# Feed-forward part of a transformer layer: where the rounding of each weight tile is traced, and two instructions that it is put behind

## The chip, the cores and the metric

One Trainium2 chip, one core. The metric is the device time of one execution in microseconds (us), the median of several runs. The profile comes from one further execution, which has its own time.

## The reference, cut to what matters

The program is one trunk layer for 640 tokens (128 context tokens, 512 latent ones) of 1024 features, in fp32: modulation from a conditioning vector, a combined input projection, grouped-query attention and neighbourhood attention, a merge, an output projection, a feed-forward part with squared ReLU, and a final norm. The change lies in the feed-forward part and the norm that ends the program:

```python
def _mlp(h, w_mlp_in, w_mlp_out):            # 1024 -> 4096 -> 1024
    return jnp.square(jax.nn.relu(h @ w_mlp_in)) @ w_mlp_out
...
h2 = _rmsnorm(x, n2) * (1 + sc2) + sh2
x = x + g2 * _mlp(h2, w1, w2)
...
y_sample = _rmsnorm(xs, final_norm_g)
```

## The kernel before, in words

**Layout.** Features lie on the 128 partitions, tokens on the free axis, in two halves of 320. An fp32 product is made of three fp32r products: each operand is a high part (a rounded copy) and a low part (the rest), and high by high, high by low and low by high are summed in one PSUM bank.

**The feed-forward part** takes the span from 557 us to about 906 us. It goes in four chunks c of 1024 hidden features. In a chunk both layers use a scheme of seven block products for a two by two block product: A11, A12, A22 and the combinations S1 to S4 of weight blocks, for n = 0 to 3 (of layer 1 the outputs, of layer 2 the pairs of output feature tiles x1_2n and x1_2n+1). The list `SEQ` (from the hand-written FIRST1, FIRST0, FIRST2, L1350 to L1366) names 196 products in the order in which they are traced. In a chunk's layer 2 that order ends S3(0..3), A22(0..3), S2(0..3), S1(0..3), S4(0..3). Each product is 12 matmuls of 128x128 by 320 columns (L1679 to L1681: high by high, high by low, low by high, four times).

**Weights.** A product's weight tile `wb` holds the high half in blocks 0 to 3 and the low half in blocks 4 to 7. Six such tiles exist, and `W.live` counts those in use. The class Operands (L1370 to L1441) fills them. `feed` loads fp32 tiles: `wst` for A11 and A12, and `wsb` for the rest, to which a GpSimd-issued DMA adds a second block of the matrix (L1401). `conv` rounds one weight: ScalarE copies to fp32r for the high half (L1416), then VectorE subtracts for the low half (L1421, for some products on GpSimd). For S4 of layer 2 in the last chunk, c = 3, ScalarE instead writes the negated weight into the low half (L1418), and a DMA issued by GpSimd adds the weight itself (L1419). After S3, S2 and A22 another GpSimd-issued DMA adds the next block into `wsb` (L1424), which forms the following combination. `ahead` rounds as long as fewer than six weights are live and the fp32 tile has been asked for.

**The main loop** (L1664 to L1709), for each product: get the weight, take a bank, 12 matmuls, then the evictions (`layer1` or `layer2`), then `W.live -= 1`, then the operands of layer 2 that have become complete (`operand` splits a hidden block into op, high on ScalarE at L1485 or L1488, low on VectorE at L1486 or L1489; `t_raw` forms sums of hidden blocks), then `ahead`, then a piece of side work. Before the loop `ahead` has rounded six weights, so that behind product i weight i+6 is rounded.

**Evictions in layer 2 of c = 3.** The bank is added with a gate into the residual tile x1 by VectorE (`gate_half`, L1532, one instruction or two, 128 and 192 columns), for S3, A22 and S2 by way of temporaries tp (L1599, L1602, L1605). When half of an x1 tile is complete, `done_half` squares it on ScalarE (L1547, tiles sq3 or acc3), adds the square to a running sum on VectorE (L1551), and scales x1 by the norm's weight on ScalarE (L1552). A half's norm is two matmuls with ones (L1559), a power on ScalarE and eight multiplications (L1568) with their output DMAs.

**What sets the order.** The program is traced in the order of the code, and the tile framework then orders each engine's instructions with its own estimates, the order of tracing as priority; so the order on an engine differs from that of the code. Within an engine instructions start in their order.

Of the kernel before, what the change touches and what calls it, by code (L numbers as in the profile page):

```python
# [74 lines left out]
def trunk_layer(ctx: ExitStack, tc: tile.TileContext, xT, small_in, wmodA, wmodB, tabs, cacheK, cacheV, bias,  # L75
                w_in, w_br, w_out, w1, w2, yT, akT, avT, bkT, bvT):
    nc = tc.nc
    PE, ACT, DVE = nc.tensor, nc.scalar, nc.vector
# [154 lines left out]
    def flush_later(todo=None):  # L233
        todo = later if todo is None else todo
        n = len(todo)
        for f in todo[:n]:
            f()
        del todo[:n]

    class Weights:  # L240
        def __init__(self):
            self.order = list(w_order())
            self.pos = {k: i for i, (k, _) in enumerate(self.order)}
            self.st, self.t = {}, {}
            self.nd = self.nc = self.live = self.busy = 0
            self.extra = self.defer = False
            self.behind = None
# [51 lines left out]
        def ahead(self):  # L299
            while self.nc < len(self.order):  # L300
                key = self.order[self.nc][0]
                if key in EXTRA and self.extra:
                    return
                if key not in EXTRA and self.live + 2 > 6:
                    return
                self.conv()
            if OPS:
                OPS[0].ahead()

    OPS = []  # L310
# [1059 lines left out]
    class Operands:  # L1370


        def __init__(self):
            self.st = {}
            self.loads = []
            for l, c, n, o in SEQ:
                k = (l, c, n, "A" if o in ("A11", "A12") else "B")
                if k not in self.loads:
                    self.loads.append(k)
            self.t = {}  # L1380
            self.nl = self.nc = 0
            self.busy = {"A": 0, "B": 0}

        def src(self, l, c, n, e):
            return (w1[8 * c + 2 * n + e] if l == 1 else w2[c, 2 * n + e]).rearrange("p (k n) -> p k n", k=KT)
# [46 lines left out]
        def ahead(self):  # L1432
            self.feed()
            while self.nc < len(SEQ) and W.live < 6 and (SEQ[self.nc][0], *SEQ[self.nc][1:3],
                                                         "A" if SEQ[self.nc][3] in ("A11", "A12") else "B") in self.st:
                self.conv()

        def get(self, x):
            while x not in self.t:
# [5 lines left out]
    def bank():  # L1445
        return pp8[0].tile([P, 512], F32, tag="b", bufs=8, name="b")[:, :HT]
# [22 lines left out]
    def opd(c, name):  # L1469
        if (c, name) not in OPD:  # L1470
            OPD[c, name] = (bp[0].tile([P, 8, HT], F32R, tag="op3", bufs=1, name="op") if len(OPD) % 3 == 2 else
                            m.tile([P, 8, HT], F32R, tag="op", bufs=2, name="op"))
        return OPD[c, name]
# [6 lines left out]
    def operand(c, name, ks=slice(0, 4)):  # L1480

        t, src = opd(c, name), hid_raw(c, {"B11": 11, "B21": 21, "T4": 21, "N22": 22}.get(name, 12))[:, ks]
        hi, lo = t[:, ks], t[:, 4 + ks.start:4 + ks.stop]
        if name == "N22":
            ACT.activation(hi, src, AF.Copy, scale=-1.0)  # L1485
            DVE.scalar_tensor_tensor(lo, src, -1.0, r32(hi), op0=OP.mult, op1=OP.subtract)  # L1486
        else:
            ACT.activation(hi, src, AF.Copy)  # L1488
            DVE.tensor_sub(lo, src, r32(hi))  # L1489

    def t_raw(c, name, ks=slice(0, 4)):

        b11, b12, b21, b22 = (hid_raw(c, b)[:, ks] for b in (11, 12, 21, 22))
        if name == "T3":
            DVE.tensor_sub(b12, b22, b12)
        elif name == "T2":
            DVE.tensor_add(b12, b12, b11)
        elif name == "T4":
            DVE.tensor_sub(b21, b21, b12)
        else:  # L1500
            DVE.tensor_sub(b12, b22, b12)
# [72 lines left out]
    def fold(n):  # L1574

        for h in range(2):
            gate_half(2 * n + 1, WS[n], h, neg)
# [58 lines left out]
    for n, h in todo:  # L1636
# [7 lines left out]
        e, i = n % 2, n // 2  # L1644
# [20 lines left out]
    for x in SEQ:  # L1665
        l, c, n, o = x
        w = OPS[0].get(x)
        if l == 1:
            xk = XN[o]
        else:  # L1670
            s = opd(c, XOF[o])
            xk = lambda k, s=s: (s[:, k], s[:, 4 + k])
        p = pairs.setdefault((l, c, n), Pair())
        whole = {"A12": "A11", "S1": "S2", "S4": "S2"}.get(o)
        b = getattr(p, "b" + whole) if whole else bank()
        setattr(p, "b" + o, b)
        for k in range(4):
            xh, xl = xk(k)
            PE.matmul(b, w[:, k], xh, start=not whole and k == 0, stop=False, skip_group_check=True)  # L1679
            PE.matmul(b, w[:, k], xl, start=False, stop=False, skip_group_check=True)  # L1680
            PE.matmul(b, w[:, 4 + k], xh, start=False, stop=o not in ("A11", "S2", "S1") and k == 3, skip_group_check=True)  # L1681
        (layer1 if l == 1 else layer2)(c, n, o, b, p)
        W.live -= 1
        if l == 1 and o in ("A12", "S2") and n > 1:
            operand(c, "B11" if o == "A12" else "B21", slice(0, 3) if n == 2 else slice(3, 4))
        if l == 1 and o == "S2":
            fold(n)
        if l == 1 and o == "S4" and n > 1:
            t_raw(c, "T3", slice(0, 3) if n == 2 else slice(3, 4))
        if l == 2:  # L1690
            if (o, n) == ("A11", 2):
                operand(c, "T3")
                t_raw(c, "T2")
                t_raw(c, "T4")
            if (o, n) == ("A11", 3):
                operand(c, "T4")
            if (o, n) == ("A12", 3):
                operand(c, "T2")
                t_raw(c, "T1")
            if (o, n) == ("S3", 3):  # L1700
                operand(c, "T1")
            if (o, n) == ("S2", 3):
                operand(c, "N22")
        OPS[0].ahead()
        flush_later()
        if side:
            side.pop(0)()
# [104 lines left out]
```

## Time and profile before

| what | value |
|---|---|
| time, median of 3 runs | 917.27 us (917.22 to 918.52) |
| profiled execution's own time | 917.51 us |
| its span in the trace | 915.7 us |
| mean granted TensorE clock | 0.997 |
| PE busy | 901.5 us, 98% of the span |
| VectorE (DVE) busy | 713.5 us, 78% |
| ScalarE (ACT) busy | 564.8 us, 62% |
| GpSimd (POOL) busy | 197.0 us, 22% |

Read it so: PE has hardly any idle time, so the other engines matter only where PE waits for them. "PEld" is the loading of a weight into PE, which overlaps the matmuls. In the timeline a row is one instruction, or several alike in a row (x2): start in us, busy us, engine, line, operation, output and inputs, count, and in brackets how long the engine was idle before it, with what ended that.

### The profile page before, as it was taken

The numbers are of one execution on the slowest core, as the hardware profiler recorded it, in microseconds if no ns is written. First come the engines' busy times: TensorE is split into PE (matmuls) and PEld (weight loads), VectorE is DVE, ScalarE is ACT, GpSimd is POOL, SyncE is SP. The second block draws the span as 40 slices with busy tenths as digits, with TensorE's granted clock in tenths as the row PEclk, the third lists the DMA queues.
The fourth block names the chain that finished last, engine by engine and source line by source line (L and its number), as shares of the span: only waits on it lengthen the run. The fifth ranks groups of instructions, "written<-read, shape, count | busy, mean of one in ns | idle before, by whom it ended". The sixth has DMA issues, their size and how long they took to land.

```text
span 915.7 us, 16620 instructions
## 1 busy us (share of the span) xinstructions
PE 901.5 (98%) x6120; PEld 871.5 (95%) x6120; DVE 713.5 (78%) x1508; ACT 564.8 (62%) x1176; POOL 197.0 (22%) x226
## 2 busy tenths in 40 slices
PE   9999999999999999999999999999999999999996
PEld 7799989999999999999999999999999999999995
DVE  6776887757666796767789996995798769976897
ACT  4566777756667765765325667537753576357765
POOL 0020200001211011211120000354244532454140
PEclk9999999999999999999999999999999999999998
DMA  9892400126645398999743463898778876898475
GB/s 348 317 266 69 113 24 26 62 72 159 161 119 125 120 284 256 249 268 251 251 140 100 116 165 105 134 210 186 186 122 191 178 174 144 180 173 182 97 126 151
DMA packets 54465, 151.09 MB, mean 165 GB/s; under 512 B 6704, under 2 KB 10432, under 8 KB 54384
## 3 DMA queue, kind: packets, MB, share of 16 engines
q1 hardware_dynamic: 31440, 99.74, 33.1%
q0 software_dynamic: 21792, 48.98, 30.8%
q10 hardware_dynamic: 1152, 1.31, 0.4%
q8 instruction: 48, 0.79, 0.4%
q14 instruction: 33, 0.27, 0.1%
HBM read 137.67 MB, written 4.60 MB: 155 GB/s over the span
## 4 chain that ended last, share of the span: by engine, by line
PE 81%; DVE 6%; DMA 5%; ACT 4%; issue 2%; POOL 0%; SPq 0%; DVEq 0%; ACTq 0%; POOLq 0%
PE b L1680 10%; PE b L1679 10%; PE b L1681 10%; PE pg L320 7%; PE pg L321 7%; PE pg L322 7%; PE pss L322 4%; PE pss L321 4%; PE pss L320 4%; DMA wsb<-w 2%; PE pt L321 2%; PE pt L322 2%; PE pt L320 2%; DMA ms<-wmodA 2%; PE pt L710 1%
## 5 line engine op out<-in xcount | busy, mean ns | idle before, releaser
L1416 ACT ACTIVATE wb<-wsb 128x512 fp32r<-128x512 f32 x140 | 87.1, 628 | 90.6 <-PE b L1681 59.2
L1680 PE MATMUL b<-op,wb 128*128 128x320 f32 x448 | 138.6, 309 | 0.7 <-DVE op L1489 0.7
L1679 PE MATMUL b<-op,wb 128*128 128x320 f32 x448 | 138.6, 309 | 0.0
L1681 PE MATMUL b<-op,wb 128*128 128x320 f32 x448 | 138.4, 309 | 0.0
L1421 DVE TENSOR_TENSOR wb<-wsb,wb 128x512 fp32r<-128x512 f32 x124 | 92.5, 749 | 26.5 <-ACT wb L1416 26.3
L1424 POOL DMA_DIRECT2D wsb<-w x84 | 74.4, 922 | 127.8 <-DVE wb L1421 99.7
L1123 DVE SCALAR_TENSOR_TENSOR mt<-wmt,cb 128x512 f32<-128x512 f32 x128 | 80.9, 686 | 6.0 <-DMA wmt<-wmodB 6.0
L1680 PEld LDWEIGHTS b<-op,wb 128*128 128x128 f32 x448 | 84.1, 188 | 1.2 <-DVE op L1489 1.2
L1679 PEld LDWEIGHTS b<-op,wb 128*128 128x128 f32 x448 | 84.1, 188 | 0.5 <-DVE x L1532 0.4
L1681 PEld LDWEIGHTS b<-op,wb 128*128 128x128 f32 x448 | 84.1, 188 | 0.0
L272 ACT ACTIVATE wh<-wst 128x512 fp32r<-128x512 f32 (+1 forms) x84 | 61.1, 739 | 32.1 <-PE pg L321 16.6
L1401 POOL DMA_DIRECT2D wsb<-w x28 | 26.0, 930 | 138.0 <-DVE xm L341 41.5
L281 DVE TENSOR_TENSOR wl<-wst,wh 128x512 fp32r<-128x512 f32 (+1 forms) x53 | 43.3, 821 | 14.9 <-ACT wh L272 12.8
L648 DVE TENSOR_TENSOR pl<-pt,ph 128x512 fp32r<-128x512 f32 (+1 forms) x72 | 44.9, 627 | 11.8 <-ACT ph L647 11.2
L647 ACT ACTIVATE ph<-pt 128x512 fp32r<-128x512 f32 (+1 forms) x72 | 39.2, 548 | 15.7 <-PE po L718 4.7
L1532 DVE SCALAR_TENSOR_TENSOR x<-b,parts,x 128x128 f32<-128x128 f32 (+1 forms) x116 | 46.3, 429 | 2.9 <-PE b L1681 2.2
L1416 ACT ACTIVATE wb<-wst 128x512 fp32r<-128x512 f32 x56 | 34.9, 626 | 17.1 <-PE b L1681 10.3
L1679 PE MATMUL b<-t,wb 128*128 128x320 f32 x144 | 44.7, 310 | 0.0
L1681 PE MATMUL b<-t,wb 128*128 128x320 f32 x144 | 44.5, 309 | 0.0
L1680 PE MATMUL b<-t,wb 128*128 128x320 f32 x144 | 44.5, 309 | 0.0
L1489 DVE TENSOR_TENSOR op<-hid,op 128x1280 fp32r<-128x1280 f32 (+2 forms) x32 | 37.0, 1155 | 7.6 <-ACT op L1488 7.4
L1532 DVE SCALAR_TENSOR_TENSOR x<-tp,parts,x 128x320 f32<-128x320 f32 (+2 forms) x60 | 38.9, 677 | 1.0 <-ACT tp L1583 1.0
(890 smaller groups left out, 3009.2 us busy)
## 6 DMA issues: line engine op xcount, KB each, us to landing
wsb<-w POOLq DMA_DIRECT2D x112, 256.0 KB, 5.1
wst<-w SPq DMA_DIRECT2D x36, 512.0 KB, 3.9
wmt<-wmodB SPq DMA_DIRECT2D x32, 512.0 KB, 5.5
wst<-w_in SPq DMA_DIRECT2D x31, 512.0 KB, 4.4
wsb<-w SPq DMA_DIRECT2D x28, 512.0 KB, 4.0
ms<-wmodA SPq DMA_DIRECT2D x16, 512.0 KB, 8.2
wl<-w_in POOLq DMA_DIRECT2D x10, 512.0 KB, 7.6
wst<-w_br SPq DMA_DIRECT2D x8, 512.0 KB, 4.2
```

The costliest lines, as they stand in the source:

```text
L272: ACT.activation(hi[:, ks], st[:, ks], AF.Copy)
L320: PE.matmul(ps, wh[:, k], xh[:, sl], start=first, stop=False)
L321: PE.matmul(ps, wh[:, k], xl[:, sl], start=False, stop=False)
L322: PE.matmul(ps, wl[:, k], xh[:, sl], start=False, stop=last)
L1123: DVE.scalar_tensor_tensor(t, st[:, q * 512:(q + 1) * 512], 1.0, r32(cb[2 * q + i][:, :512]), op0=OP.mult, op1=OP.mult, accum_out=parts[:, ...
L1416: ACT.activation(w[:, 0:4], t, AF.Copy)
L1421: (nc.gpsimd if o in BLKPOOL[l - 1] else DVE).tensor_sub(w[:, 4:8], t, r32(w[:, 0:4]))
L1424: nc.gpsimd.dma_start(t, self.src(l, c, n, e)[:, 4 * half:4 * half + 4], accum_op=OP.add)
L1532: DVE.scalar_tensor_tensor(X1[i][:, sl], src[:, sl.start - off:sl.stop - off], g[:, j:j + 1], X1[i][:, sl], op0=OP.mult, op1=OP.add)
L1679: PE.matmul(b, w[:, k], xh, start=not whole and k == 0, stop=False, skip_group_check=True)
L1680: PE.matmul(b, w[:, k], xl, start=False, stop=False, skip_group_check=True)
L1681: PE.matmul(b, w[:, 4 + k], xh, start=False, stop=o not in ("A11", "S2", "S1") and k == 3, skip_group_check=True)
```

## The change

Three edits in the feed-forward part's loop. `Operands` gets a list `behind`. Each `conv` that `ahead` makes is traced under an ordering context for each instruction in that list: what `conv` traces for an engine is put behind the listed instruction of that engine. And `ahead` is no longer called at the end of a product's turn but right after its evictions have been traced, with `behind` set to the last instruction traced until then on ScalarE and on VectorE; this is ahead of `W.live -= 1`, so that the count is still one higher, and behind product i it is weight i+5 that is rounded instead of weight i+6.

```diff
@@ class Operands, __init__
             self.busy = {"A": 0, "B": 0}
+            self.behind = []
@@ ahead
             while self.nc < len(SEQ) and W.live < 6 and (SEQ[self.nc][0], *SEQ[self.nc][1:3],
                                                          "A" if SEQ[self.nc][3] in ("A11", "A12") else "B") in self.st:
-                self.conv()
+                with ExitStack() as order:
+                    for i in self.behind:
+                        order.enter_context(tc.issue_after(i))
+                    self.conv()
@@ main loop, for x in SEQ
         (layer1 if l == 1 else layer2)(c, n, o, b, p)
+        OPS[0].behind = [next(i for i in reversed(nc.cur_bb.bb.instructions) if i.engine == e.engine) for e in (ACT, DVE)]
+        OPS[0].ahead()
         W.live -= 1
...
-        OPS[0].ahead()
         flush_later()
```

Lines after the first edit stand 1 further down in the changed kernel, from L1437 on 4 further (L1416 becomes L1417, L1547 becomes L1551), behind the third edit 6 or 5 further. All that is traced ahead of the loop keeps its order, and so do the loads that SyncE issues. Tiles of one name have other numbers in the two kernels.

The order on ScalarE near the end, in layer 2 of c = 3, before: the roundings of S1(3) (wb_10647), S4(0) (wb_10670), S4(1) (wb_10697) and S4(2) (wb_10717), with the first `done_half` behind S2, that of x1_1.

```order
L1416 ACTIVATE wb_10647<-wsb_10214 128x512
L1416 ACTIVATE wb_10670<-wsb_10205 128x512
L1418 ACTIVATE wb_10670<-wsb_10205 128x512
L1416 ACTIVATE wb_10697<-wsb_10208 128x512
L1418 ACTIVATE wb_10697<-wsb_10208 128x512
L1547 ACTIVATE sq3_10620<-x1_1_5742 128x320
L1552 ACTIVATE x1_1_5742<-x1_1_5742,pk_74 128x320
L1416 ACTIVATE wb_10717<-wsb_10211 128x512
```

The same place after, with S1(3) in wb_10667, S4(0) in wb_10690 and S4(1) in wb_10713:

```order
L1417 ACTIVATE wb_10667<-wsb_10230 128x512
L1551 ACTIVATE sq3_10686<-x1_7_6084 128x320
L1556 ACTIVATE x1_7_6084<-x1_7_6084,pk_74 128x320
L1417 ACTIVATE wb_10690<-wsb_10221 128x512
L1419 ACTIVATE wb_10690<-wsb_10221 128x512
L1551 ACTIVATE acc3_10710<-x1_1_5742 128x320
L1556 ACTIVATE x1_1_5742<-x1_1_5742,pk_74 128x320
L1417 ACTIVATE wb_10713<-wsb_10224 128x512
L1419 ACTIVATE wb_10713<-wsb_10224 128x512
```

S4(0)'s rounding stood ahead of all four `done_half` of S2, and now stands behind the last of them, that of x1_7; S4(1)'s stands behind the first square of the other half, which needs S1(0)'s eviction.

The order on VectorE around the evictions of S2, before: low halves of S1(0) to S1(3) (wb_10583, wb_10601, wb_10624, wb_10647) between the evictions of A22(2), S2(0) and S2(1) (the L1605 rows, banks b_10604 and b_10627).

```order
L1421 TENSOR_TENSOR wb_10583<-wsb_10205,wb_10583 128x512
L1602 TENSOR_TENSOR tp_10580<-b_10586,tp_10371 128x320
L1532 SCALAR_TENSOR_TENSOR x1_7_6084<-tp_10371,parts_3964,x1_7_6084 128x320
L1421 TENSOR_TENSOR wb_10601<-wsb_10208,wb_10601 128x512
L1605 TENSOR_TENSOR tp_10541<-tp_10541,b_10604 128x320
L1421 TENSOR_TENSOR wb_10624<-wsb_10211,wb_10624 128x512
L1532 SCALAR_TENSOR_TENSOR x1_1_5742<-tp_10541,parts_3964,x1_1_5742 128x128
L1532 SCALAR_TENSOR_TENSOR x1_1_5742<-tp_10541,parts_3964,x1_1_5742 128x192
L1605 TENSOR_TENSOR tp_10541<-tp_10541,b_10627 128x320
L1421 TENSOR_TENSOR wb_10647<-wsb_10214,wb_10647 128x512
```

The same place after: low halves of S1(0) (wb_10598) and S1(1) (wb_10621), and the evictions of S2(0) to S2(3) (banks b_10601, b_10624, b_10647, b_10670).

```order
L1422 TENSOR_TENSOR wb_10598<-wsb_10221,wb_10598 128x512
L1609 TENSOR_TENSOR tp_10537<-tp_10537,b_10601 128x320
L1609 TENSOR_TENSOR tp_10537<-tp_10537,b_10624 128x320
L1536 SCALAR_TENSOR_TENSOR x1_1_5742<-tp_10537,parts_3964,x1_1_5742 128x128
L1536 SCALAR_TENSOR_TENSOR x1_1_5742<-tp_10537,parts_3964,x1_1_5742 128x192
L1536 SCALAR_TENSOR_TENSOR x1_3_5901<-tp_10537,parts_3964,x1_3_5901 128x128
L1536 SCALAR_TENSOR_TENSOR x1_3_5901<-tp_10537,parts_3964,x1_3_5901 128x192
L1555 TENSOR_TENSOR acc3_10326<-acc3_10326,sq3_10617 128x320
L1609 TENSOR_TENSOR tp_10576<-tp_10576,b_10647 128x320
L1609 TENSOR_TENSOR tp_10576<-tp_10576,b_10670 128x320
L1422 TENSOR_TENSOR wb_10621<-wsb_10224,wb_10621 128x512
```

Three roundings, S1(1) to S1(3), stood ahead of the last two evictions of S2, and now stand behind them. In the rest of that stretch the rows behind these are: the running sum, the first part of x1_5, the rounding of S1(2), the second part of x1_5, x1_7, the running sum, the low half of op N22 (L1490), the rounding of S1(3).

The order on VectorE at the evictions of A12(0) and A12(1) (x1_0 and x1_2), before: low halves of A12(3) (wb_10312) and S3(0) (wb_10332).

```order
L1421 TENSOR_TENSOR wb_10312<-wst_10203,wb_10312 128x512
L1495 TENSOR_TENSOR hid12_9965<-hid22_9906,hid12_9965 128x320
L1532 SCALAR_TENSOR_TENSOR x1_0_5673<-b_10241,parts_3964,x1_0_5673 128x128
L1532 SCALAR_TENSOR_TENSOR x1_0_5673<-b_10241,parts_3964,x1_0_5673 128x192
L1421 TENSOR_TENSOR wb_10332<-wsb_10205,wb_10332 128x512
L1532 SCALAR_TENSOR_TENSOR x1_2_5824<-b_10278,parts_3964,x1_2_5824 128x128
L1532 SCALAR_TENSOR_TENSOR x1_2_5824<-b_10278,parts_3964,x1_2_5824 128x192
```

The same place after, with A11(3) in wb_10290, A12(2) in wb_10308 and A12(3) in wb_10329:

```order
L1422 TENSOR_TENSOR wb_10290<-wst_10219,wb_10290 128x512
L1528 TENSOR_TENSOR tp_10155<-tp_10155,b_10200 128x320
L1536 SCALAR_TENSOR_TENSOR x1_0_5673<-b_10238,parts_3964,x1_0_5673 128x128
L1536 SCALAR_TENSOR_TENSOR x1_0_5673<-b_10238,parts_3964,x1_0_5673 128x192
L1499 TENSOR_TENSOR hid12_9960<-hid22_9903,hid12_9960 128x320
L1422 TENSOR_TENSOR wb_10308<-wst_10105,wb_10308 128x512
L1536 SCALAR_TENSOR_TENSOR x1_2_5824<-b_10275,parts_3964,x1_2_5824 128x128
L1536 SCALAR_TENSOR_TENSOR x1_2_5824<-b_10275,parts_3964,x1_2_5824 128x192
L1493 TENSOR_TENSOR op_10374<-hid12_9960,op_10374 128x1280
L1422 TENSOR_TENSOR wb_10329<-wst_10219,wb_10329 128x512
```

At x1_2's eviction the roundings of A12(3) and S3(0) were done; now both come later, A12(3)'s behind the low half of op T3 (L1493).

On PE the order of the first product of layer 2, A11(0), and the product S1(3) of layer 1 traced after it changes in c = 1, 2 and 3: ten matmuls of A11(0), two of S1(3), the last two of A11(0), the other ten of S1(3), where before each product's twelve stood together. The same kind of change comes to S4(0) to S4(3) at the end: before twelve by twelve, after with two matmuls of the next product ahead of the last ten of each. The first half's norm matmuls (L1559, then L1563) stood between S1(3) and S4(0) and now stand behind the first two matmuls of S1(3).

On GpSimd the order at the start of layer 1 changes in c = 2 and 3: the `wsb` sum (L1401) of the chunk's second B tile stood ahead of the low half of A22(0) (L1421) and the sum behind that (L1424), and now stands behind both.

## The prediction

> **What bounds the kernel now.** I read the page first, then the waits of the feed-forward part, then windows, and last the timelines of PE, VectorE, ScalarE and GpSimd at the places that the order moves. The page gives the span and what a rounding costs; columns of a group: count, busy and mean ns of one, idle before.
>
> ```profile
> span 915.7 us, 16620 instructions
> L1416 ACT ACTIVATE wb<-wsb 128x512 fp32r<-128x512 f32 x140 | 87.1, 628 | 90.6 <-PE b L1681 59.2
> wsb<-w POOLq DMA_DIRECT2D x112, 256.0 KB, 5.1
> ```
>
> ScalarE waits 90.6 us ahead of high halves, 59.2 of it for PE, that is for one of the six weight tiles to come free: in most of the part it rounds as early as it may. The timeline of PE shows where PE itself waits (each bracket is an idle time and its end), and the two moments at which the last product and the norm end.
>
> ```profile
> 753.21 0.42 PE L1680 MATMUL b<-op,wb 128*128 128x320 f32 x1 [0.43 <-DVE op L1489]
> 852.78 0.41 PE L1680 MATMUL b<-op,wb 128*128 128x320 f32 x1 [0.28 <-DVE op L1489]
> 890.26 0.31 PE L1679 MATMUL b<-op,wb 128*128 128x320 f32 x1
> 892.02 0.31 PE L1679 MATMUL b<-op,wb 128*128 128x320 f32 x1
> 903.78 0.31 PE L1679 MATMUL b<-op,wb 128*128 128x320 f32 x1
> 905.54 0.70 PE L1559 MATMUL b<-acc,ones 128*128 128x320 f32 x2
> 907.17 0.81 PE L1559 MATMUL b<-sq,ones 128*128 128x320 f32 x2 [0.39 <-ACT sq L1547]
> ```
>
> So PE bounds the part: it idles 0.43 and 0.28 us at A11(0) of two chunks, and 0.39 in the norm. S1(0) begins at 890.26 and S1(1) at 892.02: a product takes 1.76, a matmul 0.147. S4(3) begins at 903.78. A wait elsewhere costs nothing until it uses up what the rounding is ahead by. The windows of layer 2 in c = 3 (length, then busy of PE, PEld, DVE, ACT, POOL) tell where that is least.
>
> ```profile
> 860.00:880.00 20.00, 20.00 (x138) 19.87 (x136) 19.34 (x32) 16.08 (x28) 5.70 (x7) 1.00 0.44 66
> 880.00:900.00 20.00, 20.00 (x135) 19.48 (x134) 19.37 (x41) 13.88 (x26) 8.15 (x10) 1.00 0.88 146
> ```
>
> VectorE is busy 38.7 of 40 us beside a full PE. There it runs a queue, in which a rounding's place decides, not its release.
>
> **The change part by part.** (1) One product later, and no new instruction. Every rounding that has more slack than 1.76 pays nothing. In c < 3 the last ScalarE instruction traced is mostly the rounding before, so high halves move by nothing; low halves wait behind one more eviction of VectorE, 0.4 to 0.9. The tightest one there is A22(2) in c = 2:
>
> ```profile
> 777.44 0.68 DVE L1421 TENSOR_TENSOR wb<-wsb,wb 128x512 fp32r<-128x512 f32 x1
> 779.99 0.31 PE L1679 MATMUL b<-op,wb 128*128 128x320 f32 x1
> ```
>
> It ends at 778.12 and PE comes at 779.99: 1.87 of slack against 0.9. I take 0 (bounds 0 and 0.3 a chunk).
>
> (2) A11(0). PE's order puts two matmuls of S1(3) ahead of the last two of A11(0), and these cover up to 0.29 of the wait for op: of 0.43 and 0.28 goes 0.29 and 0.28, less about 0.15 by rounding work now ahead of op in VectorE's queue in c = 1, where no wait was. I take -0.4 (bounds -0.7 and 0).
>
> (3) VectorE's queue in c = 3. The rows around x1_2's eviction, and those of the last S2 evictions:
>
> ```profile
> 861.77 0.68 DVE L1421 TENSOR_TENSOR wb<-wsb,wb 128x512 fp32r<-128x512 f32 x1
> 862.37 0.67 DVE L1532 SCALAR_TENSOR_TENSOR x<-b,parts,x 128x128 f32<-128x128 f32 x2
> 862.96 1.49 DVE L1489 TENSOR_TENSOR op<-hid,op 128x1280 fp32r<-128x1280 f32 x1
> 874.18 1.48 DVE L1489 TENSOR_TENSOR op<-hid,op 128x1280 fp32r<-128x1280 f32 x1
> 875.58 0.48 DVE L1551 TENSOR_TENSOR acc<-acc,sq 128x320 f32<-128x320 f32 x1
> 875.98 1.49 DVE L1501 TENSOR_TENSOR hid<-hid,hid 128x1280 f32<-128x1280 f32 x1
> 893.01 0.88 DVE L1605 TENSOR_TENSOR tp<-tp,b 128x320 f32<-128x320 f32 x2
> 894.00 0.49 DVE L1551 TENSOR_TENSOR acc<-acc,sq 128x320 f32<-128x320 f32 x1
> 894.41 1.27 DVE L1532 SCALAR_TENSOR_TENSOR x<-tp,parts,x 128x128 f32<-128x128 f32 x4
> ```
>
> Steps from start to start: a rounding 0.60 (861.77 to 862.37), an x1 half in two pieces 0.60 (to 862.96), a running sum 0.40 (875.58 to 875.98), a low half of op 1.40 (874.18 to 875.58), two S2 sums 0.80 (0.88 less the overlap). S2(3) ended at about 890.4, where S1(0) begins, yet is summed in the pair at 893.01: VectorE lags PE by over 2 us. After, two roundings that were done when x1_2 was evicted, A12(3) and S3(0), come later: +1.20. Three that stood ahead of the pair, S1(1) to S1(3), come behind: -1.80. With the queue full in between, the pair starts at 893.01 + 1.20 - 1.80 = 892.41. Behind it, by the order: 0.80, S1(1) 0.60, sum 0.40, the first piece of x1_5 0.26, S1(2) 0.60, the second piece 0.33 (0.26 and 0.33 share one pair's 0.60): x1_5 is done at 895.4, x1_7 0.60 later, at 896.0.
>
> On the way S3(3)'s low half stands behind two low halves of op (2.80), and S1(3)'s behind one: 896.0 + 0.40 + 1.40 + 0.60 = 898.4. PE idles there by my estimate about 1.5 and 1 us. Neither is a term of the sum, as long as (4) ends later.
>
> (4) The last weights. Their low halves go ScalarE, GpSimd, DMA; the rows of S4(1)'s rounding with the first `done_half` (L1547, L1552), S4(3)'s, a double square, and GpSimd's:
>
> ```profile
> 890.46 0.63 ACT L1416 ACTIVATE wb<-wsb 128x512 fp32r<-128x512 f32 x1 [0.61 <-PE b L1681]
> 891.00 0.62 ACT L1418 ACTIVATE wb<-wsb 128x512 fp32r<-128x512 f32 x1
> 891.52 0.46 ACT L1547 ACTIVATE sq<-x 128x320 f32<-128x320 f32 x1
> 892.00 0.56 ACT L1552 ACTIVATE x<-x,pk 128x320 f32<-128x320 f32 x1
> 892.47 0.61 ACT L1416 ACTIVATE wb<-wsb 128x512 fp32r<-128x512 f32 x1
> 894.97 0.61 ACT L1418 ACTIVATE wb<-wsb 128x512 fp32r<-128x512 f32 x1
> 899.34 0.82 ACT L1547 ACTIVATE sq<-x 128x320 f32<-128x320 f32 x2
> 895.88 0.86 POOL L1419 DMA_DIRECT2D wb<-wsb  x1 [0.88 <-PE b L1681]
> DMA to landing us min/median/max: 3.3/3.3/3.7
> ```
>
> Before, S4(3)'s negated copy ended at 895.58 (894.97 + 0.61), GpSimd started its DMA 0.30 later, and PE needed it only after 903.8. After, ScalarE takes S4(0) only behind x1_7's square and scale, and each further one behind `done_half` work of the other half. Steps: rounding 0.54, negation 0.52, square 0.48, scale 0.47, a square alone 0.41. From x1_5 at 895.4: square, scale, S1(3)'s rounding, 1.49, 896.9; x1_7's square and scale 0.95, 897.8; S4(0) 1.06, plus 0.09 to its end: 898.9. S4(1): square, scale, both roundings 2.01; S4(2): two squares, a scale, roundings, 2.42; S4(3): a scale and roundings, 1.53. The last negation ends at 904.9, the DMA starts at 905.2 and lands 3.3 later at 908.5, and ten matmuls of S4(3) that need it follow, 1.47: PE is through at 910.0 instead of 905.54, **+4.45**.
>
> What hid this before was the 8 us between S4(3)'s DMA and its use; what is late next is nothing, since the same tail follows: x1_6's eviction, square, norm, finals.
>
> ```profile
> 906.07 0.54 DVE L1532 SCALAR_TENSOR_TENSOR x<-b,parts,x 128x320 f32<-128x320 f32 x1
> ```
>
> That eviction came 0.53 after PE, behind the first half's finals on VectorE; after, more of these are done by then: -0.2 (bounds -0.4 and +0.4).
>
> Bounds of (4). If VectorE does not lag at the pair, it starts right behind S2(3), at about 890.6: 1.8 sooner, so +2.65. If the landing takes the 5.1 of the page's GpSimd issues into wsb, since `done_half` and the outputs run beside it: +1.8, so +6.25. I take 3.3, measured on this very line.
>
> PE would pause longest ahead of S4(0)'s low half, which lands at 898.9 + 0.3 + 3.3 = 902.5, while PE is there at about 898.4 + 1.47 + 0.59 = 900.5: 2.0 us. What a pause does to the clock is seen at the end:
>
> ```profile
> 910.00:912.00 2.00, 0.00 (x0) 0.00 (x0) 2.00 (x7) 0.00 (x0) 0.00 (x0) 0.77 0.76 262
> 912.00:914.00 2.00, 0.00 (x0) 0.00 (x0) 0.45 (x2) 0.00 (x0) 0.00 (x0) 0.50 1.03 359
> ```
>
> A mean granted clock of 0.77 in 910 to 912, with 0.50 from then on, puts the fall at 911.1, 3.1 after the last norm matmul's end at 907.98 (907.17 + 0.81). My pause of 2.0 stays under that, so I add nothing. The Trainium skill, "TensorE: Matmul & The Clock Gate", section "HAM oscillation — how this bites in real kernels", states that an idle gap of PE over about 3.4 us halves its clock; that agrees with 3.1 here, and by it the sum is the same until the pause is half as long again.
>
> **Sum.** +4.45 - 0.2 - 0.4 = +3.85: the profiled execution goes from 917.51 to 921.4. The median of before is 0.24 below its profiled run, so the median becomes 921.1. About 0.2%, 1.83 us, is what a measurement of this kernel can tell from no change.
>
> **Rivals.**
>
> No measurable change. VectorE catches up by S2's evictions, because the +1.20 is not there or the stalls in (3) give it time, and ScalarE's chain starts 1.8 sooner: +2.05, 919.3, and with the bounds of the A11 gain 918.9; with the squares of the other half also off the chain, as where S1's evictions come early, 2 less: 917. For it: PE's slack ahead of S4 was 8 us, and only some 4 must be lacking. Against: the order puts S4(0) behind x1_7 whatever the speed.
>
> Slower still, by GpSimd's queue. The second B tile's sum now stands behind A22(0)'s rounding and its DMA at the start of c = 2 and 3:
>
> ```profile
> 797.46 0.86 POOL L1401 DMA_DIRECT2D wsb<-w  x1 [1.39 <-DVE wb L1421]
> 800.10 0.88 POOL L1424 DMA_DIRECT2D wsb<-w  x1 [0.30 <-POOL wb L1421]
> ```
>
> It moves from 797.46 to about 800.7, 3.2 later. If the products that need it are no further ahead than A22(2) above, 1.87, they wait 1.3 in both chunks: 923.7. Against: 1.87 is the least slack that I found in c < 3, in layer 2; and PE idles nowhere in layer 1.
>
> Slower still, by the clock: the pause ahead of S4(0) exceeds 3.1, because S1(3) is not late after all, and the remaining 40 matmuls run at half rate for some of their way. Thirty at 0.147 more: +4.4, 925.5. Against: the pause is worked out as 2.0, and the first pauses take from the later one. The Trainium skill's page named above has this as its rule.
>
> Faster: nothing at the tail is late, and the A11 waits go whole, with 0.39 at the norm: -1.1, 916.2, which is still inside 0.2%. To be faster by more than 1.83 there is too little idle time on PE in the part to take away.
>
> **How the numbers follow.** The forecast has 0.66 (its own range 919.1 to 922.9, by the bounds of (4)), no measurable change 0.18, GpSimd 0.06, the clock 0.05, faster by a way that I do not see, with the small gain, 0.05. The range 917.2 to 923.6 takes in the forecast, nearly all of GpSimd's case and most of the no-change case. Slower by over 0.2%, above 919.1: 0.66 less 0.01 at its edge, plus 0.11, 0.76. Within: 0.19. Faster: 0.05.
>
> **What would show it.** In the profile after: the eviction pair of S2(2) and S2(3) on VectorE near 892.4; S4(0)'s negation ending near 898.9 and S4(3)'s near 904.9; GpSimd's last L1420 near 905.2; PE idle of 1 to 2 us, released by that DMA, ahead of S4(0), and less ahead of S4(2) and S4(3); its last S4 matmul near 909.9; idle near 875 and 897 by low halves. Wrong it would be if PE never waits for L1420's DMA, if the pauses lie in c < 3, or if the end comes by less than 1.83 later.

## The result, and the profile after

The changed kernel takes 928.85 us (median of 4 runs, 927.42 to 929.88), the kernel before 917.67 (4 runs on the same chip, the three shown above among them). The ratio is 1.0117, with a 95% interval of 1.0098 to 1.0137: slower by 10.7 us (the two medians differ by 11.2). The forecast was slower, 921.1, with 923.6 as the upper end. So the sign was right and the size too small by a factor of three.

The profiled execution took 927.42 us. Its span, and what PE waited for in the feed-forward part (columns: us in total, times, the longest):

```profile
span 925.5 us, 16598 instructions
```

```profile
PE b L1685 <- DVE wb L1422: 4.1, 5, 1.4
PE b L1685 <- DMA wb<-wsb: 2.5, 2, 1.6
PE b L1683 <- ACT op L1492: 0.6, 1, 0.6
PE b L1683 <- ACT wb L1417: 0.4, 1, 0.4
```

Before, PE waited 0.7 in this list, and only for op. Now there are 7.6, on three engines and on a DMA. The timeline of PE gives the places; the rows are the waits over 0.5, with all rows between them left out, and the last one is the norm behind the last product.

```profile
654.47 0.41 PE L1683 MATMUL b<-op,wb 128*128 128x320 f32 x1 [0.60 <-ACT op L1492]
719.49 0.41 PE L1685 MATMUL b<-hh0h,wb 128*128 128x320 f32 x1 [1.39 <-DVE wb L1422]
820.55 0.42 PE L1685 MATMUL b<-hh0h,wb 128*128 128x320 f32 x1 [0.98 <-DVE wb L1422]
881.12 0.41 PE L1685 MATMUL b<-op,wb 128*128 128x320 f32 x1 [1.08 <-DVE wb L1422]
907.55 0.41 PE L1685 MATMUL b<-op,wb 128*128 128x320 f32 x1 [1.56 <-DMA wb<-wsb]
910.47 0.42 PE L1685 MATMUL b<-op,wb 128*128 128x320 f32 x1 [0.90 <-DMA wb<-wsb]
915.27 0.70 PE L1563 MATMUL b<-acc,ones 128*128 128x320 f32 x2
```

In order: A11(0) of c = 1; A11(1) of layer 1 at the start of c = 2 and of c = 3, right ahead of S2(0) (the expectations below call these two waits S2(0)'s, the product by which the loss shows in full); S3(3) of c = 3; S4(0) and S4(1). The norm stands at 915.27 where it stood at 905.54: +9.73.

How far PE is behind the kernel before, by the start of a product in both timelines of PE:

| product | before | after | behind |
|---|---|---|---|
| A11(0), layer 2, c = 1 | 652.56 | 652.38 | -0.18 |
| A11(0), layer 1, c = 2 | 705.39 | 707.09 | 1.70 |
| S2(3), layer 1, c = 2 | 749.39 | 752.73 | 3.34 |
| A11(0), layer 1, c = 3 | 804.62 | 808.55 | 3.93 |
| S2(3), layer 1, c = 3 | 849.11 | 853.80 | 4.69 |
| S1(0), layer 2, c = 3 | 890.26 | 896.76 | 6.50 |
| norm of the second half | 905.54 | 915.27 | 9.73 |

Half of the loss, 4.7, has happened before layer 2 of c = 3 begins, where the prediction had taken 0 and even a gain of 0.4. From there on 5.0 are lost, where it had 4.45: by the starts of the products 0.6 at A11(3), 1.3 at S3(3), 2.0 at S4(0) and 1.2 at S4(1).

The tail's chain, ScalarE around S4(0) and S4(3), VectorE's pair of S2(2) and S2(3), and GpSimd's last DMA:

```profile
901.80 0.46 ACT L1551 ACTIVATE sq<-x 128x320 f32<-128x320 f32 x1
902.29 0.56 ACT L1556 ACTIVATE x<-x,pk 128x320 f32<-128x320 f32 x1
902.76 0.62 ACT L1417 ACTIVATE wb<-wsb 128x512 fp32r<-128x512 f32 x1
903.28 0.62 ACT L1419 ACTIVATE wb<-wsb 128x512 fp32r<-128x512 f32 x1
...
909.00 0.62 ACT L1419 ACTIVATE wb<-wsb 128x512 fp32r<-128x512 f32 x1
```

```profile
897.06 0.88 DVE L1609 TENSOR_TENSOR tp<-tp,b 128x320 f32<-128x320 f32 x2
```

```profile
909.91 0.86 POOL L1420 DMA_DIRECT2D wb<-wsb  x1 [0.40 <-ACT wb L1419]
```

S4(0)'s rounding stands behind x1_7's square and scale, as the order said. Its negation ends at 903.90, 5.0 later than forecast, S4(3)'s at 909.62 (+4.7), the last DMA starts at 909.91 (+4.7): the chain is the one that was worked out, moved by the 4.7 that had been lost before it. One thing differs: PE's last wait is ahead of S4(1)'s low half and not ahead of S4(3)'s. S4(1)'s DMA took 4.2 to land (906.21 to 910.43), the other three 3.3 to 3.6. S4(3)'s landed at 913.48, which with ten matmuls of 0.147 gives 914.95 by my estimate: within 0.3 of what PE did.

### The profile page after: what moved, and what is told of

Read it like the earlier page. It is cut to its first block, busy times and chain, and to the rows that moved or that the text cites. A ratio compares the mean times of both kernels' runs of the same rounds, so it can differ in the third digit from the quotient of the medians.

```text
span 925.5 us, 16598 instructions
## 1 busy us (share of the span) xinstructions
PE 903.6 (98%) x6120; PEld 871.3 (94%) x6120; DVE 708.4 (77%) x1508; ACT 561.0 (61%) x1176; POOL 197.7 (21%) x226
## 4 chain that ended last, share of the span: by engine, by line
PE 63%; DVE 17%; ACT 7%; DMA 7%; issue 5%; POOL 1%; SPq 0%; DVEq 0%; ACTq 0%; POOLq 0%
PE pg L320 7%; PE pg L321 7%; PE pg L322 7%; PE b L1685 5%; PE b L1684 4%; PE b L1683 4%; DVE wb L1422 4%; DVE x L1536 4%; PE pss L322 4%; PE pss L321 4%; PE pss L320 4%; DMA wsb<-w 3%; PE pt L322 2%; PE pt L321 2%; PE pt L320 2%
## 5 line engine op out<-in xcount | busy, mean ns | idle before, releaser
L1417 ACT ACTIVATE wb<-wsb 128x512 fp32r<-128x512 f32 x140 | 85.1, 623 | 61.1 <-DMA wsb<-w 30.1
L1422 DVE TENSOR_TENSOR wb<-wsb,wb 128x512 fp32r<-128x512 f32 x124 | 89.3, 725 | 33.4 <-ACT wb L1417 33.4
L1425 POOL DMA_DIRECT2D wsb<-w x84 | 74.4, 930 | 128.7 <-DVE wb L1422 111.6
L1422 DVE TENSOR_TENSOR wb<-wst,wb 128x512 fp32r<-128x512 f32 x44 | 32.1, 738 | 16.3 <-ACT wb L1417 16.2
L1492 ACT ACTIVATE op<-hid 128x1280 fp32r<-128x1280 f32 (+2 forms) x32 | 31.9, 998 | 18.0 <-DVE hid L1505 8.5
L1493 DVE TENSOR_TENSOR op<-hid,op 128x1280 fp32r<-128x1280 f32 (+2 forms) x32 | 37.0, 1156 | 5.8 <-ACT op L1492 5.8
```

Of the source, the lines that this page charges most:

```text
L1417: ACT.activation(w[:, 0:4], t, AF.Copy)
L1422: (nc.gpsimd if o in BLKPOOL[l - 1] else DVE).tensor_sub(w[:, 4:8], t, r32(w[:, 0:4]))
L1425: nc.gpsimd.dma_start(t, self.src(l, c, n, e)[:, 4 * half:4 * half + 4], accum_op=OP.add)
```

## The experiments

Each is measured against the kernel before on its own chip; "us" below is the ratio less one, times 917.7.

| kernel | ratio, 95% interval | us | median |
|---|---|---|---|
| the whole change | 1.0117 (1.0098 to 1.0137) | +10.7 | 928.85 |
| later_only | 1.0018 (0.9996 to 1.0040) | +1.7 | 919.31 |
| bound_only | 1.0128 (1.0112 to 1.0144) | +11.7 | 928.92 |
| layer1_only | 1.0032 (1.0019 to 1.0044) | +2.9 | 920.21 |
| mid_only | 1.0043 (1.0028 to 1.0057) | +3.9 | 921.18 |
| last_only | 1.0059 (1.0044 to 1.0074) | +5.4 | 922.07 |
| act_only | 1.0102 (1.0079 to 1.0125) | +9.4 | 926.89 |
| dve_only | 1.0152 (1.0126 to 1.0178) | +14.0 | 931.44 |
| sum_first | 1.0085 (1.0069 to 1.0101) | +7.8 | 926.23 |
| op_first_after | 1.0105 (1.0084 to 1.0127) | +9.6 | 927.00 |
| low_by_vector | 1.0067 (1.0047 to 1.0086) | +6.1 | 924.32 |
| last_dve | 1.0077 (1.0061 to 1.0094) | +7.1 | 925.90 |
| three_undone | 1.0010 (1.0001 to 1.0020) | +0.9 | 919.62 |
| op_first_before | 1.0005 (0.9995 to 1.0015) | +0.5 | 917.73 |
| low_by_vector_before | 1.0003 (0.9993 to 1.0013) | +0.3 | 917.81 |

**The two halves of the change.** The lead alone, and the binding alone:

```diff
# later_only
-        OPS[0].behind = [next(i for i in reversed(nc.cur_bb.bb.instructions) if i.engine == e.engine) for e in (ACT, DVE)]
         OPS[0].ahead()
         W.live -= 1
# bound_only
-        OPS[0].ahead()
         W.live -= 1
+        OPS[0].ahead()
```

> One half of the change alone: the rounding is traced behind the evictions of its product and with W.live one higher (five products ahead instead of six), but bound behind nothing. Theory: the loss lies in two places. At the end, S4's roundings stand behind done_half on ScalarE only by the binding; here they stand where they stood before, so the end costs nothing. In c < 3 the loss comes from chains by way of a DMA that have one product less, so most of it stays, about 3 to 5 us: 921 to 923. Rival A, the binding alone is what costs: 917.7, as before. Rival B, the lead alone is what costs: 928, as with the whole change.

> The other half alone: W.live is lowered first, so the lead stays six products, and each rounding is traced behind the evictions and bound behind them. Theory: the c < 3 losses go (GpSimd's order at a chunk's start is the old one, and S4(3)'s rounding of layer 1 no longer waits ahead of op), the end stays late, but less than with the whole change, since S4(0) stands behind x1_5's done_half and no longer behind x1_7's: one done_half and one rounding less, 1.5 us, from the 4.8 that the whole change loses in layer 2 of c = 3: +3, 920.7 (919.5 to 922). Rival A, the binding alone is what costs: 928. Rival B, the lead alone: 917.7.

The lead alone can hardly be told from the kernel before. The binding alone costs as much as the whole change. So both theories about c < 3 fell: the losses there are the binding's. In bound_only PE, with the lead unchanged, loses 3.9 from the start of the feed-forward part to the end of layer 1 of c = 3. The places are in part others than in the changed kernel: 1.0 goes in layer 1 of c = 1, and 1.2 at A11(0) of c = 1, as in the changed kernel. The timelines of its ScalarE and GpSimd show why A11(0) waits:

```profile
653.63 0.63 ACT L1417 ACTIVATE wb<-wsb 128x512 fp32r<-128x512 f32 x1 [0.75 <-DMA wsb<-w]
...
655.52 0.45 ACT L1492 ACTIVATE op<-hid 128x320 fp32r<-128x320 f32 x1
```

```profile
648.43 0.86 POOL L1425 DMA_DIRECT2D wsb<-w  x1 [0.71 <-DVE tp L1525]
```

The sum that S2(3)'s rounding starts (L1425) goes out at 648.43; before, it went out at 644.24, and PE is only 1.5 behind by then. S4(3)'s rounding waits for it on ScalarE, and op, which A11(0) needs, is queued behind that rounding. In the changed kernel it is the same, with the sum at 647.59:

```profile
653.42 0.63 ACT L1417 ACTIVATE wb<-wsb 128x512 fp32r<-128x512 f32 x1 [1.19 <-DMA wsb<-w]
653.96 0.45 ACT L1492 ACTIVATE op<-hid 128x320 fp32r<-128x320 f32 x1
```

**By place.** The change switched on by a condition on the product, and otherwise the old call at the end of the turn:

```diff
+        new = l == 1            # layer1_only;  l == 2 and c < 3: mid_only;  (l, c) == (2, 3): last_only
+        OPS[0].behind = []
+        if new:
             OPS[0].behind = [...]
             OPS[0].ahead()
         W.live -= 1
...
+        if not new:
+            OPS[0].ahead()
         flush_later()
```

> The whole change in the products of layer 1 only; layer 2's products round as before. Theory: layer 1 holds the stalls that the trace of after shows at A11(0) of c = 1 (1.0, op behind a rounding that waits for a DMA) and at S2(0) of c = 2 and 3 (1.64 and 1.25). The second needs the chunk's second B tile late on GpSimd, and that order is only partly changed here (its sum stands behind the rounding of A22(0) but ahead of the sum behind that), so 1.0 plus half of 2.9: +2.5, 920.2 (918.5 to 921.6). Rival, everything that was lost lies in layer 2: 917.7.

> The whole change in layer 2 of c = 0, 1 and 2 only, which closes the account by place: layer 1 alone gave +2.85, layer 2 of c = 3 alone +4.7, and the whole change +11.2. Theory: the places add up, +3.6: the order of GpSimd's sums at a chunk's start is set by the roundings that are traced at the end of layer 2 and comes with this part (2.9 of stalls at S2(0)), and A22(1) and A22(2) of c = 1 and 2 take 0.6 each: 921.4 (920 to 923). Rival, the parts lose more together than each alone: 918.5 or less.

> The whole change in layer 2 of the last chunk, c = 3, only. Theory, the steps (3) and (4) of the prediction: +4.45 less what the tail gains, 4.3, so 922.0; the trace of after gives 4.8 for this stretch, 922.5. Rival, the lateness at the end comes from what was lost before it: under +2, below 919.7.

All three came out at the size that the theory had: +2.9, +3.9, +5.4, together 12.2 against 10.7 for the whole, inside the intervals. The last place is steps (3) and (4) of the prediction, whose sum was +4.3 with its tail; that part stands. The other two came out by other waits than the theory had, so their fit is in part luck. In layer1_only PE loses 1.7 at A11(0) of c = 1 and nothing at the start of c = 2 and 3. In mid_only A22 of c = 1 and 2 loses nothing, and the loss at the start of c = 2 and 3 shows as two waits of PE for banks that VectorE has not emptied, and not for a rounding:

```profile
PEld b L1683 <- DVE tp L1522: 4.0, 2, 2.2
```

Behind the second of these, an idle time of PE of 1.94, the granted clock was 0.52 and 0.63 in the windows 826 to 828 and 828 to 830, which cost about 1.5 of the 4.1 that PE loses in this profile.

**Which engine's binding.** In the list of engines after `for e in`, one is left out:

```diff
-... for e in (ACT, DVE)]
+... for e in (ACT,)]        # act_only;  (DVE,): dve_only;  last_dve: (DVE,) in layer 2 of c = 3, else both
```

> The changed kernel, bound behind ScalarE's last eviction instruction only. A low half needs its high half, so VectorE's order hardly changes by leaving its binding out. Theory: it is the binding on ScalarE that costs, at the end by done_half and in c = 1 by the rounding ahead of op: 928.5 (927 to 930). Rival, VectorE's binding costs: 920 to 922.

> The changed kernel, bound behind VectorE's last eviction instruction only. ScalarE's S4 roundings stand ahead of done_half again, as with the lead alone. Theory: as the lead alone plus what VectorE's eviction order and GpSimd's order at the chunks' start cost, 919.3 + 1.5: 921 (919 to 923). Rival, VectorE's binding costs: 928.

> The changed kernel, with ScalarE's binding left out in layer 2 of c = 3 alone (VectorE's stays, with its evictions and S2's pair ahead of the roundings of S1(1) to S1(3)). ScalarE then rounds S4(0) and S4(1) ahead of done_half again. Theory, step (4): it is done_half ahead of S4's roundings on ScalarE that makes the end late, so the S4 part, 3 to 4 us, goes: 925.3 (924 to 926.5). Rival, VectorE's binding makes S2's evictions and S1's low halves late, and the end with them: 928 or more.

act_only nearly reproduces the change, though its profile holds a fall of the clock as well (below). last_dve takes 3.6 of the loss away, and in its trace PE loses 0.2 at each of S4(0) and S4(1), where the changed kernel loses 2.0 and 1.2: ScalarE's binding, by done_half, makes the last weights late. dve_only missed both expectations and is the slowest of all, for two reasons. The first is the order: ScalarE has S4(3)'s rounding of layer 1 in front of both relus again, as in the kernel before, where the changed kernel has it behind them, while VectorE's binding makes S2(3)'s low half, and with it the sum, later. The timeline of its ScalarE in c = 2, and the same rounding in the kernel before:

```profile
757.49 0.63 ACT L1417 ACTIVATE wb<-wsb 128x512 fp32r<-128x512 f32 x1 [3.72 <-DMA wsb<-w]
...
760.22 0.47 ACT L1492 ACTIVATE op<-hid 128x320 fp32r<-128x320 f32 x1
```

```profile
749.07 0.63 ACT L1416 ACTIVATE wb<-wsb 128x512 fp32r<-128x512 f32 x1 [2.04 <-DMA wsb<-w]
```

A rounding that waits 3.72 for its sum holds up op, and PE waits for op at A11(0) in each of the three chunks:

```profile
PEld b L1683 <- ACT op L1492: 6.1, 3, 2.5
```

The kernel before has the same wait of this rounding for its sum, 2.04 long: this is where its own idle time at A11(0), quoted in the prediction, came from.

The second reason is the clock. Behind each of these three waits (PE idle for 1.33, 2.23 and 1.72) the granted clock falls to half. The windows behind the first, with length, busy of PE, PEld, DVE, ACT and POOL, then the clock:

```profile
656.00:658.00 2.00, 1.50 (x5) 1.28 (x6) 1.46 (x5) 1.94 (x5) 0.00 (x0) 0.72 0.35 115
658.00:660.00 2.00, 2.00 (x9) 2.00 (x8) 1.55 (x3) 0.81 (x2) 0.00 (x0) 0.50 0.89 258
660.00:662.00 2.00, 2.00 (x14) 2.00 (x14) 1.09 (x2) 0.64 (x2) 0.86 (x1) 0.92 0.93 287
```

By the starts of the products PE loses 7.4 at the three A11(0) and 4.3 more right behind them, at half rate. All four runs of dve_only have a lower mean clock (0.991 to 0.996) than the runs of before on that chip (0.997 and 0.998). So about 4 of its 14.0 are the clock's, by estimate, and not the order's.

**One mechanism at a time.** The sum of a chunk's second B tile put back ahead of A22(0)'s rounding on GpSimd; S4(3)'s rounding of layer 1 behind op's high half on ScalarE; S4's last low halves by VectorE:

```diff
# sum_first: in ahead, for (l, n, o) == (1, 0, "A22") and c > 1
-                    for i in self.behind:
+                    for i in self.behind + [self.sum[l, c, 1]]:
# op_first_after, op_first_before: for (l, n, o) == (1, 3, "S4") and c > 0, not before A12(3)'s operand is traced
+                    order.enter_context(tc.issue_after(self.op[c]))
# low_by_vector, low_by_vector_before
-LOTAIL = tuple(("S4", n) for n in range(4))
+LOTAIL = ()
```

> The changed kernel, with one order put back on GpSimd: at the start of layer 1 in c = 2 and 3 the rounding of A22(0) is bound behind the sum that forms the chunk's second B tile, as it stood before. Theory (the GpSimd rival of the prediction): the stalls of 1.64 and 1.25 us at S2(0) come from that sum, which delays S3(1)'s rounding, the VectorE queue behind it and two GpSimd roundings: they go, -2.9, 926.0 (925 to 927). Rival, the stall comes from VectorE's binding alone: no change, 928.9.

By the ratio it came out as the theory had it, +7.8 instead of +10.7, with intervals that just overlap. The trace shows less. First the changed kernel's timelines at the start of c = 3, GpSimd and VectorE, and the sum's row of GpSimd in sum_first:

```profile
804.91 2.08 POOL L1402 DMA_DIRECT2D wsb<-w  x2
...
814.96 3.19 POOL L1422 TENSOR_TENSOR wb<-wst,wb 128x512 fp32r<-128x512 f32 x2
```

```profile
811.99 0.69 DVE L1422 TENSOR_TENSOR wb<-wsb,wb 128x512 fp32r<-128x512 f32 x1 [1.42 <-ACT wb L1417]
812.60 1.41 DVE L1536 SCALAR_TENSOR_TENSOR x<-tp,parts,x 128x128 f32<-128x128 f32 x1
813.93 0.54 DVE L1536 SCALAR_TENSOR_TENSOR x<-b,parts,x 128x320 f32<-128x320 f32 x1
814.39 5.50 DVE L1536 SCALAR_TENSOR_TENSOR x<-tp,parts,x 128x192 f32<-128x192 f32 x5
819.81 0.68 DVE L1422 TENSOR_TENSOR wb<-wst,wb 128x512 fp32r<-128x512 f32 x1
```

```profile
801.66 0.86 POOL L1403 DMA_DIRECT2D wsb<-w  x1 [1.22 <-DVE wb L1424]
```

The second tile's sum goes out at 804.91 (in sum_first at 801.66). S3(1)'s low half comes at 811.99 (2.2 later than in sum_first, 809.76, where PE is 1.3 less behind), and x1 updates of the chunk before stand behind it on VectorE. They then meet two GpSimd roundings in a row and take 5.50 us for five: the first of them alone takes 3.98, from 814.39 to 818.37, and the roundings end at 818.15. A11(1)'s low half, 819.81, comes after all of them; PE goes on with it at 820.55.

But sum_first has the same meeting, with VectorE's rows again:

```profile
812.50 5.52 DVE L1540 SCALAR_TENSOR_TENSOR x<-tp,parts,x 128x192 f32<-128x192 f32 x5
817.95 0.68 DVE L1424 TENSOR_TENSOR wb<-wst,wb 128x512 fp32r<-128x512 f32 x1
```

PE still loses 0.80 and 0.66 at A11(1) of c = 2 and 3 there, where the changed kernel loses 1.65 and 1.24. So putting the sum back takes away 1.4 of these 2.9, about half. Even that half is not safely the sum's: op_first_after below leaves the sum late, and loses 0.87 and 0.65 at the same products. That A11(1)'s low half is late behind the x1 updates is shown; how much of it the sum's place causes stays open.

> The changed kernel with the same move: S4(3)'s rounding of layer 1 stands behind the high half of op B11 on ScalarE. Theory: the loss of 1.0 us at A11(0) in c = 1 goes and what is left of the waits in c = 2 and 3 with it, -1.5, 927.4 (926.4 to 928.3). Rival, op's high half is late by the binding of the evictions ahead of it: no change, 928.9.

The median is 1.9 lower; by the ratio it is 1.1, inside the interval of the whole change, so the time alone does not decide. The trace does, for this wait: PE's wait at A11(0) of c = 1, 2 and 3 is gone, and PE is 0.1 behind there (0.35 when c = 1 begins its layer 2, 0.49 after A11), where the changed kernel lost 1.2. (The profiled execution is the fastest of its four, 923.58 to 929.56.)

> The kernel before, with one rounding moved: S4(3) of layer 1 in c = 1 to 3 is rounded behind the high half of op B11 on ScalarE, where it stood ahead of the relu that op needs and waited there 2.04 us for a sum's DMA in c = 2. Theory, that wait is what made PE idle at A11(0) of c = 2 and 3 (1.25 us in all with the slower steps around it): PE no longer waits there, -1.0, 916.4 (915.8 to 917.2). Rival, op is late by VectorE: no change, 917.4.

The list of PE's waits has no entry of the feed-forward part left, only the norm's:

```profile
PE b L1567 <- ACT sq L1555: 1.0, 1, 1.0
```

From A11 of c = 1 to S4(3) PE gained 1.6 us in the traces (0.63 behind at first, 0.94 ahead at the end), 1.2 of it at the two A11(0), but the norm's square came 0.6 later behind PE, and the median is that of before, where 1.0 less was expected: an effect under 0.15%, which this measurement doesn't show. So the wait's cause is shown, and a faster kernel is not.

> The changed kernel, with the low halves of the last four weights (S4 of layer 2, c = 3) made by VectorE's subtraction as everywhere else, instead of a negated copy on ScalarE and a DMA. Theory, step (4): the negations (0.52 each), GpSimd's 0.3 and the landing of 3.3 leave the chain, the last low half is there at about the time of before, so that most of the end's 4.8 goes: 925.0 (924 to 926.5). Rival, the end is late by what was lost before it and by VectorE's evictions, and not by this chain: 928.9 or more.

> The kernel before, with the last four low halves made by VectorE instead of a negated copy and a DMA: what this edit does without the change. Theory: S4's low halves had 8 us of slack, four subtractions of 0.60 on a full VectorE cost at most that much: 917.4 to 918.5, so that the 4.5 us that the same edit took off the changed kernel come from the chain at its end. Rival, the edit is a gain by itself: 914 or less.

4.6 less in the changed kernel, nothing in the kernel before: at the end, the chain of negation, GpSimd and landing is what PE waits for. In low_by_vector no DMA is left among PE's waits:

```profile
PE b L1685 <- DVE wb L1422: 3.5, 4, 1.6
PE b L1683 <- ACT op L1492: 1.5, 2, 0.8
PE b L1683 <- ACT wb L1417: 0.7, 1, 0.7
PE b L1685 <- POOL wb L1422: 0.4, 1, 0.4
```

> The changed kernel with three mechanisms undone together and the change itself left in place: the second tile's sum ahead of A22(0)'s rounding on GpSimd, S4(3)'s rounding of layer 1 behind op's high half on ScalarE, and the last four low halves made by VectorE. Theory: the three are all that matters but for 0.6 us each at A22 of c = 1 and 2 and the waits at S3 of c = 3, so they add up: 928.9 - 2.6 - 1.9 - 4.5 = 919.9 (918.9 to 922). Rival, the product less of lead costs by itself wherever something is tight, and a wait that is undone shows up at the next place: 924 or more.

All three at once, with the change left in: +0.9 (0.1 to 1.8). They add up within the intervals, 2.9 + 1.1 + 4.6 = 8.6 singly, 9.8 together. The stall at the start of c = 2 is gone here, that at the start of c = 3 is not (0.8). What is left on PE is one line, A22(1) of c = 2, the start of c = 3 and S3(3):

```profile
PE b L1692 <- DVE wb L1424: 1.7, 3, 0.9
```

## Why the prediction was wrong, step by step

**Step (1) failed: "I take 0 (bounds 0 and 0.3 a chunk)" for all of c < 3 and layer 1.** PE lost 4.7 to 4.9 there. The step looked at one rounding, the low half with the least slack, and moved it by one eviction. It did not ask what stands behind a rounding on its engine, nor what its DMA starts. Three things were missed. S2(3)'s rounding starts the sum that S4(3)'s rounding waits for, and that one stands ahead of op on ScalarE: 1.2 at A11(0) in c = 1. A22(1)'s low half in c = 1 and 2 went behind a low half of op and a hidden sum, two of 1.4, and not behind one eviction: 0.6 each. In c = 2, VectorE and the matmul of PE that waits:

```profile
778.68 1.49 DVE L1493 TENSOR_TENSOR op<-hid,op 128x1280 fp32r<-128x1280 f32 x1
780.09 0.49 DVE L1590 TENSOR_TENSOR tp<-tp,b 128x320 f32<-128x320 f32 x1
780.48 1.49 DVE L1505 TENSOR_TENSOR hid<-hid,hid 128x1280 f32<-128x1280 f32 x1
781.88 0.70 DVE L1422 TENSOR_TENSOR wb<-wsb,wb 128x512 fp32r<-128x512 f32 x1
```

```profile
782.63 0.41 PE L1685 MATMUL b<-op,wb 128*128 128x320 f32 x1 [0.30 <-DVE wb L1422]
```

The third is A11(1)'s low half at the start of c = 2 and 3, behind x1 updates that meet two GpSimd roundings: 1.6 and 1.2.

**The GpSimd rival had the place and the size of a real loss, and at most half of its cause** (1.3 in both chunks; PE's rows show 1.39 and 0.98, and with the steps around them it fell 1.6 and 1.2 behind). With the sum back in its place, 0.8 and 0.7 of that remain, so the fit of the price is in part luck. The rival was given 0.06, as another way the change could go. But it shared no condition with the forecast: nothing in (4) made it less likely, and its reordering could be read in the order. As far as it holds, it was a term of the sum that was booked as a rival. The reason given against it, that PE idles nowhere in layer 1 before, says nothing about a tile that comes 3.2 later.

**Step (2) had the wrong sign.** The two matmuls of S1(3) do cover part of the wait for op, but op comes later, by the rounding that waits. In c = 2 and 3 next to nothing is gained (0.0 and 0.2), and in c = 1 there is the loss of 1.2 that is counted above: about +1.0 in all, where -0.4 was taken.

**Step (3) was half right.** S3(3)'s wait is there, 1.08 against an estimate of 1.5. That VectorE would lag at S2's pair by 2 us did not hold: PE itself was 6.5 late, and the pair at 897.06 comes right behind S2(3)'s end. Less the 4.7 lost earlier, that is 892.4, the forecast start. It came out for another reason: 1.8 of PE's lateness arose in this layer, at A11(3) and S3(3), and stood in for the lag that was missing. Without that the prediction's own lower bound, +2.65, would have been the one to take; that (4) begins at the right time is partly luck. S1(3)'s forecast wait is not there.

**Step (4) was right in its chain,** with the start just told and a last wait at S4(1) where S4(3) was forecast. +4.45 was worked out, last_only measured +5.4 (4.0 to 6.8) and the trace of the whole change 5.0 for that stretch. The two experiments that it rests on, done_half off ScalarE's way and the DMA out of the chain, took 3.6 and 4.6 away.

**The clock.** The pause ahead of S4(0) was forecast as 2.0 and is 1.56. "I add nothing" held for the whole change, where the granted clock stays 1.00. It did not hold for last_only, whose pause is as long:

```profile
902.39 0.41 PE L1685 MATMUL b<-op,wb 128*128 128x320 f32 x1 [1.54 <-DMA wb<-wsb]
```

```profile
902.00:904.00 2.00, 1.61 (x8) 1.62 (x8) 0.23 (x1) 2.00 (x5) 0.51 (x1) 0.73 0.76 131
904.00:906.00 2.00, 2.00 (x9) 2.00 (x9) 0.95 (x2) 1.19 (x3) 1.22 (x2) 0.50 0.61 106
906.00:908.00 2.00, 2.00 (x15) 2.00 (x14) 0.54 (x2) 1.42 (x4) 0.00 (x0) 0.92 0.93 156
```

The mean of 0.73 puts the fall to half at 902.9, after PE had started again, and the 0.92 its end at 906.3: 3.4 us at half rate, 1.7 lost, though S4's chain would have held PE up for a part of it. The 5.4 of last_only does not rest on this: its other three runs have a mean clock of 0.998 against 0.996 here, and took 921.36 to 923.08 against 922.54.

Over all profiles the clock fell behind pauses of 1.33 (with another of 0.48 one matmul later), 1.72 and 2.23 (dve_only), 1.54 (last_only), 1.55 (act_only and op_first_after) and 1.94 (mid_only). It did not fall behind 1.39 and 1.56 (the whole change), 1.51 (last_dve), 1.55 (sum_first), 1.56 (bound_only and low_by_vector) and 1.57 (mid_only, the first). So the prediction's step from 3.1 was wrong as a reading: the 3.1 is how long PE had been idle when the clock fell at the end, and not the shortest pause that a fall can follow. Each of the pauses here from 1.72 on was followed by one, and the forecast pause was 2.0. That the whole change lost nothing to the clock in its profile is luck.

The Trainium skill, "TensorE: Matmul & The Clock Gate", section "HAM oscillation — how this bites in real kernels", has it that gaps over about 3.4 us do this. The runs disagree: 1.54 was enough once, 1.55 twice and once not, and 1.56 was never enough. Why is open.

## What to carry to other kernels

To put a piece of work behind another on an engine that runs in order is to put it ahead of all that comes after: ask of each moved instruction what it starts (a DMA whose landing another engine waits for in its queue), and what stands behind it while it waits. Check every place where an order changes by what it delays, not only the place with the least slack. And two mechanisms that don't exclude each other are terms of one sum, however unlikely one looks, and not rivals.

## What the runs showed of the hardware

In the changed kernel an x1 update of 192 columns on VectorE took 3.98 beside two GpSimd roundings (814.39 on, above), and ended 0.2 after them. The other four of its row took 0.34 to 0.54 each. The row of the 3.98, and four updates in a row, of 128 and 192 columns, with no rounding on GpSimd:

```profile
814.39 3.98 DVE L1536 SCALAR_TENSOR_TENSOR x<-tp,parts,x 128x192 f32<-128x192 f32 x1
```

```profile
895.42 1.28 DVE L1536 SCALAR_TENSOR_TENSOR x<-tp,parts,x 128x128 f32<-128x128 f32 x4
```

The Trainium skill, "Perfetto Trace Analysis", section "Optimizing Scalar/DVE Operations", says that GpSimd and VectorE share a read port in SBUF, and that a VectorE operation which uses two ports holds it as an exclusive lock. The rows agree that the two get in each other's way; here it was VectorE's update that was held up, for about as long as both roundings took (3.19).

The second point is the clock, told above: pauses of PE of 1.33 to 2.23 were followed by half rate in some executions, for 3.4 us in the one that is worked out, so that a pause can cost more than its length.
